# Half of the gate and up projections of two FFNs by seven half products instead of eight, on one Trainium2 core

## The chip, the cores and the metric

The kernel runs on one core of one Trainium2 chip. The metric is the device time of one execution in microseconds (us), a median over runs. One further execution was profiled; every duration and every row below is from that one. Engines are named as the profile names them: PE (TensorE, matmuls), PEld (its weight loads, which overlap the matmuls), DVE (VectorE), ACT (ScalarE), POOL (GpSimd) and SP (SyncE, which here only issues the DMAs).

## The reference, cut to what matters

Two layers, each a mixer and then a SwiGLU feed-forward network (FFN); the change is in the FFNs, which have 1024 model columns, 2816 inner columns and 512 tokens.

```python
def swiglu(h, w1, w3, w2):
    return (jax.nn.silu(h @ w1) * (h @ w3)) @ w2

for layer in range(DEPTH):                 # DEPTH = 2
    ...
    x = x + mix.astype(x.dtype)
    h = rmsnorm(x, norm_ffn_g[layer])
    x = x + swiglu(h, ffn_w1[layer], ffn_w3[layer], ffn_w2[layer]).astype(x.dtype)
```

All of it is float32.

## The kernel before

Activations are kept transposed: `xT[k]` holds 128 model columns (partitions) by 512 tokens, k = 0 to 7. A float32 product is made of three reduced-precision matmuls: each operand is split into a rounded part (`hh`, `whi`, `gh`: a cast on ACT, L116 for weights, L154 for activations) and what is left (`hl`, `wlo`, `gl`: a subtraction on DVE, L118 and L155), and PE adds wh·xh, wh·xl and wl·xh (L129, L130, L131). The RMS norm's factor per token, `R`, is applied after the projection.

The inner columns of an FFN are 22 tiles of 128, f = 0 to 21. For each f there is a pair of projections, the gate `a` and the up `b`. The weights of each come as one DMA of 512 KB into a buffer `raw` (two buffers for both), are split in two pieces of 512 columns into `whi` and `wlo` (five buffers each), and are multiplied in 8 blocks of 128 x 128 against 512 tokens, so 24 matmuls of 512 columns for `a` and 24 for `b`. Then come `ta` = a·R (DVE, L259), its silu (ACT, L260), `g` = b·ta (DVE, L262), g·R (POOL, L263) and the split of g into `gh` and `gl`. `ta` and `g` are in the shared temporaries of tag "t", of which there are four.

The 22 pairs go in two halves of 11. After each half, `residual_out` multiplies its 11 g tiles by `w2` for all 8 output tiles m and adds the result to `xT[m]` (L238); what the trace calls `y` is this. In the last FFN the last output tile is done in two parts of 256 tokens, the only 256-column matmuls against these operands.

The order of instructions on each engine is set by a scheduler that works on the whole program; each engine then runs its list in order, and waits at each instruction for what it needs. The functions that the diff touches follow.

Of the kernel before, what the change touches and what calls it, by code (L numbers as in the profile page):

```python
# [24 lines left out]
NF = DFF // 128  # L25
# [6 lines left out]
def trunk(ctx, tc, t_in, out):  # L32
    nc = tc.nc
    main = ctx.enter_context(tc.tile_pool(name="main", bufs=1))
    wp = ctx.enter_context(tc.tile_pool(name="wp", bufs=2))
# [16 lines left out]
    def temp(name, dt=F32):
        return tmp.tile([128, 512], dt, name=name, tag="t")
# [69 lines left out]
    def accumulate(o, ws, width, xs, first, last, j0=0):  # L123
        n = len(xs)
        for j, (xh, xl) in enumerate(xs):
            hi, lo = ws[(j0 + j) * width // 512]
            c = (j0 + j) * width % 512
            wh, wl = hi[:, c:c + width], lo[:, c:c + width]
            mm(o, wh, xh, start=first and j == 0, stop=False)  # L129
            mm(o, wh, xl, start=False, stop=False)  # L130
            mm(o, wl, xh, start=False, stop=last and j == n - 1)  # L131

    def project(src, name, width=128, tag="mm"):
        o = bank(tag, f"p_{name}")
# [91 lines left out]
    def residual_out(wsrc, k0, k1, xs, norm, name, tail=None):  # L226
        for m in range(KT):
            o = bank("sc" if m % 2 else "mm", f"{name}{m}")
            ws = []
            for c0 in range(k0, k1, 8):  # L230
                n = min(8, k1 - c0)
                ws.append((c0, n, load_split(wsrc[m, :, c0 * 128:(c0 + n) * 128], n * 128, f"{name}{m}_{c0}")))
            parts = [slice(0, S)] if tail is None or m < KT - 1 else [slice(0, 256), slice(256, 512)]
            for cs in parts:
                for c0, n, w in ws:
                    accumulate(o[:, cs], w, 128, [(a[:, cs], b[:, cs]) for a, b in xs[c0:c0 + n]],
                               c0 == k0, c0 + n == k1)
                nc.vector.tensor_tensor(out=xT[m][:, cs], in0=o[:, cs], in1=xT[m][:, cs], op=ALU.add)  # L238
                if norm is not None:
                    norm.take(m, cs)  # L240
                    if tail is not None:
                        norm.scale(m, cs)
                if len(parts) > 1:
                    tail(cs)

    def ffn(layer, norm, norm_next, tail=None):
        w13, w2 = t_in["w13"], t_in["w2"]
        bh = [slab(i, f"gh{layer}_{i}", FR) for i in range(2)]
        bl = [slab(2 + i, f"gl{layer}_{i}", FR) for i in range(2)]
        gs = [(bh[f // 4][:, f % 4, :], bl[f // 4][:, f % 4, :]) for f in range(8)]  # L250
        gs += [(cell(2 * f - 16, f"gh{layer}_{f}", FR), cell(2 * f - 15, f"gl{layer}_{f}", FR))
               for f in range(8, NF)]
        for f0, f1 in ((0, NF // 2), (NF // 2, NF)):
            for f in range(f0, f1):
                a = project(w13[layer, 2 * f], f"a{layer}_{f}")
                R = norm.R if norm.R is not None else norm.factor()
                b = project(w13[layer, 2 * f + 1], f"b{layer}_{f}", tag="sc")
                ta = temp(f"ta{layer}_{f}")
                nc.vector.tensor_tensor(out=ta, in0=a, in1=R, op=ALU.mult)  # L259
                nc.scalar.activation(out=ta, in_=ta, func=AF.Silu)  # L260
                g = temp(f"g{layer}_{f}")
                nc.vector.tensor_tensor(out=g, in0=b, in1=ta, op=ALU.mult)  # L262
                nc.gpsimd.tensor_tensor(out=g, in0=g, in1=R, op=ALU.mult)  # L263
                split(*gs[f], g)
# [27 lines left out]
    ws = load_split(w0[5], D, "v1")  # L292
# [697 lines left out]
```

## Time and profile before

| what | value |
|---|---|
| median of 3 runs | 1332.17 us (1331.62 to 1332.23) |
| profiled execution, its own time | 1332.36 us |
| its span, first to last instruction | 1330.6 us |
| TensorE clock granted, mean | 0.999 of full speed |
| PE busy | 1317.5 us (99%) |
| PEld busy | 1102.5 us (83%) |
| DVE busy | 706.0 us (53%) |
| ACT busy | 523.1 us (39%) |
| POOL busy | 357.4 us (27%) |

The time is the span and 1.8 us around it. Busy shares are averages over the whole span; the first FFN lies at about 306 to 670 us of it, the second at about 958 to 1324 us.

### The profile page before, as it was taken

The numbers are of one execution on the slowest core, as the hardware profiler recorded it, in microseconds if no ns is written. First come the engines' busy times: TensorE is split into PE (matmuls) and PEld (weight loads), VectorE is DVE, ScalarE is ACT, GpSimd is POOL, SyncE is SP. The second block draws the span as 40 slices with busy tenths as digits, with TensorE's granted clock in tenths as the row PEclk, the third lists the DMA queues.
The fourth block names the chain that finished last, engine by engine and source line by source line (L and its number), as shares of the span: only waits on it lengthen the run. The fifth ranks groups of instructions, "written<-read, shape, count | busy, mean of one in ns | idle before, by whom it ended". The sixth has DMA issues, their size and how long they took to land.

```text
span 1330.6 us, 17637 instructions
## 1 busy us (share of the span) xinstructions
PE 1317.5 (99%) x6593; PEld 1102.5 (83%) x6593; DVE 706.0 (53%) x1252; ACT 523.1 (39%) x975; POOL 357.4 (27%) x373
## 2 busy tenths in 40 slices
PE   9999999999999999999999999999999999999998
PEld 8888888888888888888888888888788888888887
DVE  6637776854444334444469777764744433344432
ACT  5346656543333223333343344332533322333343
POOL 0116676321111001111147665551211100011111
PEclk9999999999999999999999999999999999999999
DMA  7741111032333343323322212221323323333332
GB/s 260 179 139 49 32 49 48 17 101 90 95 98 94 89 147 96 95 85 103 97 80 89 71 56 72 64 67 61 111 82 99 104 83 110 95 96 95 92 93 85
DMA packets 40373, 121.95 MB, mean 92 GB/s; under 512 B 5408, under 2 KB 9952, under 8 KB 40160
## 3 DMA queue, kind: packets, MB, share of 16 engines
q1 hardware_dynamic: 40144, 120.57, 29.7%
q8 instruction: 52, 0.85, 0.3%
q10 hardware_dynamic: 144, 0.26, 0.1%
q14 instruction: 33, 0.27, 0.1%
HBM read 113.47 MB, written 2.10 MB: 87 GB/s over the span
## 4 chain that ended last, share of the span: by engine, by line
PE 80%; DVE 1%; issue 1%; POOL 1%; ACT 0%; POOLq 0%; DVEq 0%; ACTq 0%
PE p_b L129 6%; PE p_b L131 6%; PE p_a L131 6%; PE p_a L129 6%; PE p_a L130 6%; PE p_b L130 6%; PE y L129 6%; PE y L130 6%; PE y L131 6%; PE mo L129 2%; PE mo L130 2%; PE mo L131 2%; PE lv L787 2%; PE p_hg L130 1%; PE p_hg L131 1%; PE p_hg L129 1%
## 5 line engine op out<-in xcount | busy, mean ns | idle before, releaser
L263 POOL TENSOR_TENSOR g<-g,R 128x512 f32<-128x512 f32 x44 | 70.0, 1592 | 517.8 <-DVE g L262 517.8
L129 PE MATMUL y<-gh,whi_y 128*128 128x512 f32 (+1 forms) x363 | 139.0, 383 | 0.0
L131 PE MATMUL y<-gh,wlo_y 128*128 128x512 f32 (+1 forms) x363 | 138.3, 383 | 0.0
L130 PE MATMUL y<-gl,whi_y 128*128 128x512 f32 (+1 forms) x363 | 138.2, 383 | 0.0
L129 PE MATMUL p_b<-hh,whi_b 128*128 128x512 f32 x352 | 137.1, 390 | 0.0
L130 PE MATMUL p_a<-hl,whi_a 128*128 128x512 f32 x352 | 137.1, 390 | 0.0
L131 PE MATMUL p_b<-hh,wlo_b 128*128 128x512 f32 x352 | 137.0, 389 | 0.0
L129 PE MATMUL p_a<-hh,whi_a 128*128 128x512 f32 x352 | 136.9, 389 | 0.0
L131 PE MATMUL p_a<-hh,wlo_a 128*128 128x512 f32 x352 | 136.9, 389 | 0.0
L130 PE MATMUL p_b<-hl,whi_b 128*128 128x512 f32 x352 | 136.9, 389 | 0.0
L118 DVE TENSOR_TENSOR wlo_y<-raw_y,whi_y 128x512 fp32r<-128x512 f32 (+1 forms) x96 | 62.6, 652 | 95.9 <-ACT whi_y L116 95.9
L116 ACT CAST whi_y<-raw_y 128x512 fp32r<-128x512 f32 (+1 forms) x96 | 56.3, 586 | 144.1 <-PE y L130 102.0
L118 DVE TENSOR_TENSOR wlo_b<-raw_b,whi_b 128x512 fp32r<-128x512 f32 x88 | 62.8, 714 | 87.4 <-ACT whi_b L116 87.3
L116 ACT CAST whi_b<-raw_b 128x512 fp32r<-128x512 f32 x88 | 54.6, 621 | 125.5 <-issue 56.4
L116 ACT CAST whi_a<-raw_a 128x512 fp32r<-128x512 f32 x88 | 54.5, 619 | 98.7 <-PE p_b L130 71.1
L130 PEld LDWEIGHTS y<-gl,whi_y 128*128 128x128 f32 x363 | 68.2, 188 | 13.4
L129 PEld LDWEIGHTS y<-gh,whi_y 128*128 128x128 f32 x363 | 68.2, 188 | 13.3
L131 PEld LDWEIGHTS y<-gh,wlo_y 128*128 128x128 f32 x363 | 68.2, 188 | 13.2
L131 PEld LDWEIGHTS p_b<-hh,wlo_b 128*128 128x128 f32 x352 | 66.1, 188 | 13.8
L130 PEld LDWEIGHTS p_b<-hl,whi_b 128*128 128x128 f32 x352 | 66.1, 188 | 13.7
L130 PEld LDWEIGHTS p_a<-hl,whi_a 128*128 128x128 f32 x352 | 66.1, 188 | 13.7
L129 PEld LDWEIGHTS p_a<-hh,whi_a 128*128 128x128 f32 x352 | 66.1, 188 | 13.7
(379 smaller groups left out, 2998.8 us busy)
## 6 DMA issues: line engine op xcount, KB each, us to landing
raw_a<-w SPq DMA_DIRECT2D x44, 512.0 KB, 3.5
raw_b<-w SPq DMA_DIRECT2D x44, 512.0 KB, 3.6
raw_y<-w SPq DMA_DIRECT2D x32, 512.0 KB, 3.5
raw_mo<-w_out SPq DMA_DIRECT2D x16, 512.0 KB, 3.7
raw_r<-w_in SPq DMA_DIRECT2D x12, 512.0 KB, 3.6
raw_y<-w SPq DMA_DIRECT2D x32, 192.0 KB, 2.4
raw_hf<-w_in SPq DMA_DIRECT2D x8, 512.0 KB, 3.6
raw_hq<-w_in SPq DMA_DIRECT2D x8, 512.0 KB, 3.5
```

What stands on the lines that cost most here:

```text
L116: nc.scalar.copy(hi[:, :m], part)
L118: lo_eng[c // 512 % len(lo_eng)].tensor_tensor(out=lo[:, :m], in0=part, in1=hi[:, :m].bitcast(F32), op=ALU.subtract)
L129: mm(o, wh, xh, start=first and j == 0, stop=False)
L130: mm(o, wh, xl, start=False, stop=False)
L131: mm(o, wl, xh, start=False, stop=last and j == n - 1)
L263: nc.gpsimd.tensor_tensor(out=g, in0=g, in1=R, op=ALU.mult)
L787: mm(s_[:M, c * 64:(c + 1) * 64].rearrange("p (a b) -> p a b", b=B), k[:, c * 128:c * 128 + M], q4[:, c * nb:(c + 1) * nb, 1, :], start=Tr ...
```

## The change

Of the 22 pairs of each layer, eleven (`SEVEN`) are computed in another way. The two weight tiles a and b (128 inner columns each) are cut along the contraction into a first and a second half (a1, a2, b1, b2: 4 blocks of 128 x 128 each), and the activations along the tokens into the first and second 256. The two-by-two product of halves is then made from seven products instead of eight (Strassen's identity in Winograd's form), each of 4 blocks against 256 tokens.

- `seven_operands`, once per layer ahead of f = 2, forms the sums and differences of activations that four of the seven products need, for k = 0 to 3: `x1` and `x2` (ACT), `xu` and `xw` (DVE, four operations of 256 columns) and their splits. It uses the same four temporaries "t".
- `seven_products`, for each f in `SEVEN`, loads both weight tiles, forms four sums of weight halves s1 to s4 (DVE, 128 x 512), splits seven weight operands where a pair split four, makes 7 x 12 = 84 matmuls of 256 columns, and puts the results together in operations of 256 columns. `p1` is copied by ACT.
- The gated activations of the second half of the FFN now go where those of the first half were, so `residual_out` counts its tiles from k0, `lraw` (a mask's staging area, loaded in the first FFN) moves from slab 0 to slab 4, and the place of `yout` changes.

```diff
-                    accumulate(o[:, cs], w, 128, [(a[:, cs], b[:, cs]) for a, b in xs[c0:c0 + n]],
+                    accumulate(o[:, cs], w, 128, [(a[:, cs], b[:, cs]) for a, b in xs[c0 - k0:c0 - k0 + n]],
...
+    SEVEN = [2, 4, 6, 8, 10, 11, 13, 15, 17, 19, 21]
+    def seven_operands(layer, which):
+        lo, hi = slice(0, 256), slice(256, 512)
+        xs = {1: [], 2: [], 3: [], 4: [], 5: [], 6: [], 7: []}
+        for k in range(4):
+            x1, x2 = temp(f"x1_{layer}_{k}"), temp(f"x2_{layer}_{k}")
+            for x, j in ((x1, k), (x2, k + 4)):
+                nc.scalar.activation(out=x, in_=xT[j], func=AF.Copy, scale=gains[:, which, j:j + 1])
+            u, w = temp(f"xu_{layer}_{k}"), temp(f"xw_{layer}_{k}")
+            tt = nc.vector.tensor_tensor
+            tt(out=u[:, lo], in0=x1[:, lo], in1=x1[:, hi], op=ALU.subtract)
+            tt(out=u[:, hi], in0=x2[:, hi], in1=u[:, lo], op=ALU.add)
+            tt(out=w[:, lo], in0=x2[:, lo], in1=u[:, hi], op=ALU.subtract)
+            tt(out=w[:, hi], in0=x1[:, hi], in1=x2[:, hi], op=ALU.subtract)
...
+            split(*U, u)
+            split(*W, w)
+            for i, part, cs in ((1, (hh[k], hl[k]), lo), (2, (hh[k + 4], hl[k + 4]), lo),
+                                (3, (hh[k + 4], hl[k + 4]), hi), (5, U, lo), (6, U, hi), (4, W, lo), (7, W, hi)):
+                xs[i].append((part[0][:, cs], part[1][:, cs]))
+        return xs
...
+        def product(i, o, first):
+            ((wh_, wl_),) = ws[i]
+            for j, (xh, xl) in enumerate(xs[i]):
+                wh, wl = wh_[:, j * 128:(j + 1) * 128], wl_[:, j * 128:(j + 1) * 128]
+                mm(o, wh, xh, start=first and j == 0, stop=False, skip_group_check=True)
+                mm(o, wh, xl, start=False, stop=False, skip_group_check=True)
+                mm(o, wl, xh, start=False, stop=j == 3, skip_group_check=True)
...
+        parts(1, a1)
+        tt(out=s1, in0=b1, in1=b2, op=ALU.add)
+        tt(out=s2, in0=s1, in1=a1, op=ALU.add)
+        o1 = bank("mm", f"p_w{name}")[:, lo]
+        product(1, o1, True)
+        nc.scalar.copy(p1, o1)
+        parts(6, s2)
+        o2 = bank("sc", f"p_x{name}")[:, lo]
+        product(6, o2, True)
+        parts(2, a2)
+        tt(out=v, in0=o2, in1=p1, op=ALU.subtract)
+        tt(out=s3, in0=a1, in1=b1, op=ALU.add)
+        product(2, o1, False)
+        parts(7, s3)
+        product(7, o2, False)
+        parts(5, s1)
+        tt(out=v7, in0=o2, in1=p1, op=ALU.subtract)
+        tt(out=s4, in0=s2, in1=a2, op=ALU.add)
+        o3 = bank("sc", f"p_z{name}")[:, lo]
+        product(5, o3, True)
+        parts(4, b2)
+        product(4, o2, False)
+        tt(out=g[:, hi], in0=v7, in1=o3, op=ALU.subtract)
+        parts(3, s4)
+        product(3, o3, False)
+        R = norm.R
+        tt(out=ta[:, lo], in0=o1, in1=R[:, lo], op=ALU.mult)
+        tt(out=g[:, lo], in0=o2, in1=p1, op=ALU.subtract)
+        tt(out=ta[:, hi], in0=o3, in1=v, op=ALU.subtract)
+        tt(out=ta[:, hi], in0=ta[:, hi], in1=R[:, hi], op=ALU.mult)
+        nc.scalar.activation(out=ta, in_=ta, func=AF.Silu)
+        tt(out=g, in0=g, in1=ta, op=ALU.mult)
+        nc.gpsimd.tensor_tensor(out=g, in0=g, in1=R, op=ALU.mult)
...
+                if f == 2:
+                    xs = seven_operands(layer, norm.which)
+                if f in SEVEN:
+                    g = seven_products(layer, f, xs, norm, SEVEN.index(f))
```

Two places of the engines' lists show where the new work stands. In the order lists, `g0_1` is the g of layer 0, f = 1; `wlo_s5_0_2` is the low part of the weight operand of product 5 of layer 0, f = 2; `xu_0_k` and `xw_0_k` are the temporaries of `seven_operands`, and `xu0_k_0` and `xu0_k_1` the rounded and the low part of xu (the number at the end of a name counts buffers).

The first place is DVE's list behind the last result of f = 1 of layer 0. Before, the weights of the next pairs were split there:

```order
L262 TENSOR_TENSOR g0_1_3668<-p_b0_1_3630,ta0_1_3665 128x512
L118 TENSOR_TENSOR wlo_a0_3_0_3756<-raw_a0_3_3752,whi_a0_3_0_3754 128x512
L155 TENSOR_TENSOR gl0_0_3471<-g0_1_3668,gh0_0_3469 128x512
L118 TENSOR_TENSOR wlo_a0_3_512_3760<-raw_a0_3_3752,whi_a0_3_512_3758 128x512
L259 TENSOR_TENSOR ta0_2_3743<-p_a0_2_3673,R1_3550 128x512
```

Now, from the same instruction on (its line is L360):

```order
L360 TENSOR_TENSOR g0_1_3646<-p_b0_1_3608,ta0_1_3643 128x512
L118 TENSOR_TENSOR wlo_s5_0_2_0_3805<-s_0_2_3727,whi_s5_0_2_0_3803 128x512
L260 TENSOR_TENSOR xu_0_0_3655<-x1_0_0_3651 128x256
L261 TENSOR_TENSOR xu_0_0_3655<-x2_0_0_3652,xu_0_0_3655 128x256
L118 TENSOR_TENSOR wlo_s4_0_2_0_3824<-raw_b0_2_3724,whi_s4_0_2_0_3822 128x512
L155 TENSOR_TENSOR gl0_0_0_3471<-g0_1_3646,gh0_0_0_3469 128x512
L155 TENSOR_TENSOR xu0_0_1_3662<-xu_0_0_3655,xu0_0_0_3661 128x512
L262 TENSOR_TENSOR xw_0_0_3656<-x2_0_0_3652,xu_0_0_3655 128x256
L263 TENSOR_TENSOR xw_0_0_3656<-x1_0_0_3651,x2_0_0_3652 128x256
L118 TENSOR_TENSOR wlo_s3_0_2_0_3841<-s_0_2_3727,whi_s3_0_2_0_3839 128x512
L260 TENSOR_TENSOR xu_0_1_3673<-x1_0_1_3669 128x256
L155 TENSOR_TENSOR xw0_0_1_3664<-xw_0_0_3656,xw0_0_0_3663 128x512
```

The operands of `seven_operands` have moved in behind `g0_1`, for k = 0 and the start of k = 1; k = 2 and 3 follow in the same manner. On PE, products 1 and 2 of f = 2, which need no such operand, come first, and then products 6 (into `p_x`) and 5 (into `p_z`) alternate, k by k:

```order
L298 MATMUL p_w0_2_3738<-hh7_81,wlo_s2_0_2_0_3771 128x256
L296 MATMUL p_x0_2_3756<-xu0_0_0_3661,whi_s6_0_2_0_3752 128x256
L296 MATMUL p_z0_2_3809<-xu0_0_0_3661,whi_s5_0_2_0_3803 128x256
L297 MATMUL p_x0_2_3756<-xu0_0_1_3662,whi_s6_0_2_0_3752 128x256
L298 MATMUL p_x0_2_3756<-xu0_0_0_3661,wlo_s6_0_2_0_3754 128x256
L297 MATMUL p_z0_2_3809<-xu0_0_1_3662,whi_s5_0_2_0_3803 128x256
L298 MATMUL p_z0_2_3809<-xu0_0_0_3661,wlo_s5_0_2_0_3805 128x256
L296 MATMUL p_x0_2_3756<-xu0_1_0_3679,whi_s6_0_2_0_3752 128x256
```

Before, PE had there the 48 matmuls of the pair f = 2 with operands that are long made; now each group of six stands behind the xu of its k.

The second place is DVE's list between a pair of seven products and the next one, here f = 4 and f = 6 of layer 0, with the plain pair f = 5 between them (the pattern repeats through both layers). Before, DVE did per pair four weight splits, ta, g and gl:

```order
L118 TENSOR_TENSOR wlo_b0_5_512_3951<-raw_b0_5_3943,whi_b0_5_512_3949 128x512
L262 TENSOR_TENSOR g0_4_3902<-p_b0_4_3864,ta0_4_3899 128x512
L118 TENSOR_TENSOR wlo_a0_6_0_3990<-raw_a0_6_3986,whi_a0_6_0_3988 128x512
L155 TENSOR_TENSOR gl0_1_3472<-g0_4_3902,gh0_1_3470 128x512
L118 TENSOR_TENSOR wlo_a0_6_512_3994<-raw_a0_6_3986,whi_a0_6_512_3992 128x512
L259 TENSOR_TENSOR ta0_5_3977<-p_a0_5_3907,R1_3550 128x512
L118 TENSOR_TENSOR wlo_b0_6_0_4025<-raw_b0_6_4021,whi_b0_6_0_4023 128x512
```

Now the stretch up to the low part of s5 of f = 6 reads:

```order
L118 TENSOR_TENSOR wlo_s1_0_6_0_4175<-raw_a0_6_4164,whi_s1_0_6_0_4173 128x512
L305 TENSOR_TENSOR s_0_6_4168<-s_0_6_4168,raw_a0_6_4164 128x512
L331 TENSOR_TENSOR ta0_4_3952<-p_z0_4_4031,t1_0_4_3950 128x256
L357 TENSOR_TENSOR ta0_5_4156<-p_a0_5_4086,R1_3528 128x512
L320 TENSOR_TENSOR s_0_6_4168<-s_0_6_4168,raw_a0_6_4164 128x512
L332 TENSOR_TENSOR ta0_4_3952<-ta0_4_3952,R1_3528 128x256
L118 TENSOR_TENSOR wlo_s6_0_6_0_4195<-s_0_6_4168,whi_s6_0_6_0_4193 128x512
L118 TENSOR_TENSOR wlo_s2_0_6_0_4212<-raw_a0_6_4164,whi_s2_0_6_0_4210 128x512
L118 TENSOR_TENSOR wlo_s7_0_6_0_4230<-s_0_6_4168,whi_s7_0_6_0_4228 128x512
L334 TENSOR_TENSOR g0_4_3953<-g0_4_3953,ta0_4_3952 128x512
L360 TENSOR_TENSOR g0_5_4159<-p_b0_5_4121,ta0_5_4156 128x512
L118 TENSOR_TENSOR wlo_s5_0_6_0_4246<-s_0_6_4168,whi_s5_0_6_0_4244 128x512
```

Directly ahead of these rows stand the two weight sums L304 and L314, which wait for the loads of f = 6; ahead of them L330 (256 columns) and the low part of the second piece of b of f = 5, after which that piece's `raw` buffer is free for b of f = 6. L334 and L360 are each followed on POOL by a multiplication of their g by R (L335, L361). What moved: thirteen operations of DVE now stand between the arrival of b of f = 6 and the low part of s5, where a low part before stood directly behind its own cast. On PE the matmuls of this stretch go in the order products 1, 6, 5, 2 and 7 of f, 22 of the 24 matmuls of a of f + 1, products 4 and 3 of f, the last two of a, and the 24 of b of f + 1.

## Rows read from the trace of the kernel before

**Rows 1.** Page, part 1: busy time, share of the span.

```profile
PE 1317.5 (99%) x6593; PEld 1102.5 (83%) x6593; DVE 706.0 (53%) x1252; ACT 523.1 (39%) x975; POOL 357.4 (27%) x373
```

**Rows 2.** Windows: from:to, length, busy of each engine, PEclk, DMA share, GB/s.

```profile
306.00:670.00 364.00, 364.00 (x1616) 301.63 (x1615) 152.40 (x232) 120.60 (x200) 43.83 (x29) 1.00 0.33 99
958.00:1324.00 366.00, 366.00 (x1680) 305.38 (x1678) 142.23 (x223) 120.78 (x200) 44.51 (x30) 1.00 0.31 93
```

**Rows 3.** Timeline of PE: one pair in 512-column matmuls (start us, duration us).

```profile
485.45 0.39 PE L129 MATMUL p_a<-hh,whi_a 128*128 128x512 f32 x1
485.67 0.39 PE L130 MATMUL p_a<-hl,whi_a 128*128 128x512 f32 x1
...
490.89 0.39 PE L129 MATMUL p_b<-hh,whi_b 128*128 128x512 f32 x1
...
496.33 0.39 PE L129 MATMUL p_a<-hh,whi_a 128*128 128x512 f32 x1
```

**Rows 4.** Timeline of PE: the first and the last of 23 matmuls of 256 columns.

```profile
1319.09 0.28 PE L130 MATMUL y<-gl,whi_y 128*128 128x256 f32 x1
...
1321.72 0.29 PE L131 MATMUL y<-gh,wlo_y 128*128 128x256 f32 x1
```

**Rows 5.** Timeline of DVE: one pair of the first FFN; idle before, releaser in brackets.

```profile
499.65 0.69 DVE L155 TENSOR_TENSOR gl<-g,gh 128x512 fp32r<-128x512 f32 x1 [1.84 <-ACT gh L154]
500.26 0.68 DVE L118 TENSOR_TENSOR wlo_a<-raw_a,whi_a 128x512 fp32r<-128x512 f32 x1
501.97 0.69 DVE L259 TENSOR_TENSOR ta<-p_a,R 128x512 f32<-128x512 f32 x1 [1.02 <-PE p_a L131]
...
505.17 0.69 DVE L118 TENSOR_TENSOR wlo_b<-raw_b,whi_b 128x512 fp32r<-128x512 f32 x1 [1.91 <-ACT whi_b L116]
```

**Rows 6.** Timeline of ACT, the same stretch.

```profile
504.51 0.62 ACT L116 CAST whi_b<-raw_b 128x512 fp32r<-128x512 f32 x1 [1.19 <-PE p_b L130]
...
509.88 0.62 ACT L154 CAST gh<-g 128x512 fp32r<-128x512 f32 x1 [2.03 <-POOL g L263]
510.41 0.61 ACT L116 CAST whi_a<-raw_a 128x512 fp32r<-128x512 f32 x1
```

**Rows 7.** Timeline of SP: the issue of a weight load.

```profile
505.89 0.33 SPq L109 DMA_DIRECT2D raw_b<-w  x1
```

**Rows 8.** Page, part 6: DMA issues, KB each, us from issue to landing.

```profile
raw_b<-w SPq DMA_DIRECT2D x44, 512.0 KB, 3.6
```

**Rows 9.** Groups by form: count, busy us, mean ns, idle before.

```profile
L238 DVE TENSOR_TENSOR xall<-y,xall 128x256 f32<-128x256 f32 x2 | 0.8, 424 | 6.4 <-PE y L131 6.4
L118 DVE TENSOR_TENSOR wlo_b<-raw_b,whi_b 128x512 fp32r<-128x512 f32 x88 | 62.8, 714 | 87.4 <-ACT whi_b L116 87.3
L260 ACT ACTIVATE ta<-ta 128x512 f32<-128x512 f32 x44 | 27.8, 632 | 13.4 <-DVE ta L259 13.3
```

**Rows 10.** Timeline of PE: first matmuls of f = 2, first FFN.

```profile
327.69 0.39 PE L129 MATMUL p_a<-hh,whi_a 128*128 128x512 f32 x1
```

**Rows 11.** Timeline of DVE at the start of the first FFN.

```profile
323.19 0.68 DVE L259 TENSOR_TENSOR ta<-p_a,R 128x512 f32<-128x512 f32 x1
323.79 1.40 DVE L118 TENSOR_TENSOR wlo_b<-raw_b,whi_b 128x512 fp32r<-128x512 f32 x1
...
327.89 0.69 DVE L262 TENSOR_TENSOR g<-p_b,ta 128x512 f32<-128x512 f32 x1 [1.27 <-PE p_b L131]
328.49 0.68 DVE L118 TENSOR_TENSOR wlo_a<-raw_a,whi_a 128x512 fp32r<-128x512 f32 x1
```

**Rows 12.** Timeline of POOL, the same stretch.

```profile
323.35 1.28 POOL L263 TENSOR_TENSOR g<-g,R 128x512 f32<-128x512 f32 x1 [9.52 <-DVE g L262]
328.66 1.67 POOL L263 TENSOR_TENSOR g<-g,R 128x512 f32<-128x512 f32 x1 [4.02 <-DVE g L262]
```

**Rows 13.** Windows at the end of the program, columns as in rows 2.

```profile
1324.00:1328.00 4.00, 0.08 (x1) 0.00 (x0) 1.41 (x3) 1.26 (x2) 0.69 (x1) 1.00 0.50 202
1328.00:1330.60 2.60, 0.00 (x0) 0.00 (x0) 0.00 (x0) 0.00 (x0) 0.00 (x0) 0.50 0.41 161
```

More of the change, by code (lines that the diff above doesn't have):

```diff
@@ L244, in residual_out @@
                     tail(cs)
+    SEVEN = [2, 4, 6, 8, 10, 11, 13, 15, 17, 19, 21]
[12 more added lines that the diff above has]
+            tt(out=w[:, hi], in0=x1[:, hi], in1=x2[:, hi], op=ALU.subtract)
+            U, W = ([cell(6 + 4 * k + 2 * j + i, f"x{n}{layer}_{k}_{i}", FR) for i in range(2)]
+                    for j, n in enumerate("uw"))
+            split(*U, u)
[4 more added lines that the diff above has]
+        return xs
@@ new lines, in seven_products, with parts @@
+    def seven_products(layer, f, xs, norm, n):
+        w13 = t_in["w13"]
+        lo, hi = slice(0, 256), slice(256, 512)
+        tt = nc.vector.tensor_tensor
+        name = f"{layer}_{f}"
+        ra, rb = (wp.tile([128, 1024], F32, name=f"raw_{x}{name}", tag="raw", bufs=2) for x in "ab")
+        nc.sync.dma_start(out=ra, in_=w13[layer, 2 * f])
+        nc.sync.dma_start(out=rb, in_=w13[layer, 2 * f + 1])
+        a1, a2, b1, b2 = ra[:, 0:512], ra[:, 512:1024], rb[:, 0:512], rb[:, 512:1024]
+        if n % 2:
+            s1, s2, s3, s4 = (cell(22 + j, f"s{j}_{name}") for j in range(4))
+        else:
+            q = slab(4, f"s_{name}")
+            s1, s2, s3, s4 = (q[:, j, :] for j in range(4))
+        ws = {}
+        def parts(i, src):
+            ws[i] = load_split(None, 512, f"s{i}_{name}", [src])
+        def product(i, o, first):
[5 more added lines that the diff above has]
+                mm(o, wl, xh, start=False, stop=j == 3, skip_group_check=True)
+        t1, t2 = cell(26, f"t1_{name}"), cell(27, f"t2_{name}")
+        p1, v, v7 = t1[:, lo], t1[:, hi], t2[:, lo]
+        ta, g = temp(f"ta{name}"), temp(f"g{name}")
+        parts(1, a1)
[31 more added lines that the diff above has]
+        nc.gpsimd.tensor_tensor(out=g, in0=g, in1=R, op=ALU.mult)
+        return g
@@ L246, in ffn @@
     def ffn(layer, norm, norm_next, tail=None):
         w13, w2 = t_in["w13"], t_in["w2"]
[L248 to L253, printed above, removed]
-            for f in range(f0, f1):
[L255 to L264, printed above, removed]
+        half = NF // 2
@@ new lines, in ffn @@
+        for f0, f1 in ((0, half), (half, NF)):
+            bh = [slab(i, f"gh{layer}_{f0}_{i}", FR) for i in range(2)]
+            bl = [slab(2 + i, f"gl{layer}_{f0}_{i}", FR) for i in range(2)]
+            gs = [(bh[j // 4][:, j % 4, :], bl[j // 4][:, j % 4, :]) for j in range(8)]
+            gs += [(cell(2 * j, f"gh{layer}_{f0}_{j}", FR), cell(2 * j + 1, f"gl{layer}_{f0}_{j}", FR))
+                   for j in range(half - 8)]
+            for f in range(f0, f1):
+                if f == 2:
+                    xs = seven_operands(layer, norm.which)
+                if f in SEVEN:
+                    g = seven_products(layer, f, xs, norm, SEVEN.index(f))
+                else:
+                    a = project(w13[layer, 2 * f], f"a{layer}_{f}")
+                    R = norm.R if norm.R is not None else norm.factor()
+                    b = project(w13[layer, 2 * f + 1], f"b{layer}_{f}", tag="sc")
+                    ta = temp(f"ta{layer}_{f}")
+                    nc.vector.tensor_tensor(out=ta, in0=a, in1=R, op=ALU.mult)
+                    nc.scalar.activation(out=ta, in_=ta, func=AF.Silu)
+                    g = temp(f"g{layer}_{f}")
+                    nc.vector.tensor_tensor(out=g, in0=b, in1=ta, op=ALU.mult)
+                    nc.gpsimd.tensor_tensor(out=g, in0=g, in1=R, op=ALU.mult)
+                split(*gs[f - f0], g)
@@ L685, in trunk @@
     lmask = tmp.tile([128, 8, 256], U8, name="lmask", tag="pct", bufs=2)
-    lraw = slab(0, "lraw").rearrange("p a b -> p (a b)")[:, 0:2048]
+    lraw = slab(4, "lraw").rearrange("p a b -> p (a b)")[:, 0:2048]
     nc.sync.dma_start(out=lraw, in_=t_in["lmask"].rearrange("p a b -> p (a b)"))
@@ L882, in finish @@
         c0, c1 = cs.start // 128, cs.stop // 128
-        y = slab(c0 // 2, f"yout{c0}").rearrange("p (c e) n -> p c (e n)", e=2)
+        y = slab(0 if c0 else 4, f"yout{c0}").rearrange("p (c e) n -> p c (e n)", e=2)
         banks = {(c, e): bank("oo" if e and c % 2 == 0 else "sc" if e else "mm", f"yt{c}_{e}")
```

## The prediction

> **What bounds the kernel now.** I read the page's busy shares first: PE is busy 99% of the span [rows 1]. The windows over the two FFNs say where the change stands: in both PE has no idle at all, at full granted clock, while DVE works 152.40 of 364 us and 142.23 of 366, ACT a third, POOL an eighth [rows 2]. So a matmul less is time less, as long as every other engine keeps up; and nothing else that is made cheaper there would show. Then the timelines: each matmul of 512 columns is drawn 0.39 us long, but they overlap, so the pace is read from starts. A pair begins at 485.45, its b at 490.89, the next pair at 496.33 [rows 3]: 10.88 us for 48, 0.2267 each. The same operands in 256-column matmuls start at 1319.09 and, 22 steps on, at 1321.72 [rows 4]: 0.1195 each.
>
> **What the change removes on PE.** Per pair 48 matmuls at 0.2267 (10.88 us) become 84 at 0.1195 (10.04 us): 0.84 us less, and 18.4 us for 22 pairs. One eighth of the products goes, but 256 columns cost 53% of 512, not half; that takes 0.52 of the 1.36 us. If nothing ever waited, 1332.4 (the profiled execution; 0.2 over the median) would become 1314.0, and that is the bound of the gain.
>
> The Trainium skill ("TensorE: Matmul & The Clock Gate", section "Back-to-back issue gap") gives an isolated gap of columns/2.4 + 2.5 ns: by estimate 109 and 216 ns, where the rows have 119.5 and 226.7. By it the saving would be 1.18 us per pair and 26 us in all. The rows were measured on this kernel's operands and decide.
>
> **What it adds at f = 2, twice (once per layer).** Before, PE began f = 2 at 327.69 [rows 10]; I walk the new program from there in the first FFN. PE does products 1 and 2 (2.9 us), which need no new operand, and then products 6 and 5, which for each k wait for xu of that k and its low part. If all were ready, the four products would end 48 x 0.1195 = 5.74 us on, at 333.4. But xu and xw use the temporaries that f = 0 and f = 1 held, and stand on DVE behind g of f = 1 (order rows at the first place), which cannot start before b of f = 1 ends: 327.89 [rows 11].
>
> Durations: DVE 512 columns 0.69 with the next start 0.60 behind (499.65 and 500.26 [rows 5]); 256 columns 0.42 [rows 9], so about 0.34 to the next; ACT 0.62 with 0.53 [rows 6]. The low part of s5 starts at 328.5. POOL's multiplication of that g was put at 328.66, behind a DVE operation, and took 1.67 [rows 12], so to 330.33. The first xu operation reads only SBUF, and such an operation does not run beside POOL: wlo_b, begun at 323.79 with POOL at work from 323.35, took 1.40 instead of 0.68, while ta, which reads PSUM, took its usual 0.68 [rows 11, 12]. So xu of k = 0 begins at about 330.3 and is whole at 331.0. The low parts of s4, xu 0 and s3, gl and xw fill DVE to 334.1; xu of k = 1 is whole at 335.4.
>
> From there each k takes this: cast of xu on ACT (0.05 after it, 0.53), x1 of the next k in the temporary just left (0.62), the first xu operation (0.34), the low part of xw, which stands ahead of the second one (0.60), and that (0.34): 2.7 us with the handovers. So k = 3 is whole at 340.9, its cast at 341.6, its low part at 342.3, and the last matmuls of products 6 and 5 end at 342.8. Product 7 writes the bank that v is still to be taken from, and v stands behind the low part of xw of k = 3: 343.9, instead of 333.9 with two matmuls of a between. That is 10 us of PE per layer, 20 for both. The bound from below is DVE's own work, 4 x (4 x 0.34 + 2 x 0.60) = 10.2 us from 329.1 on, so 6 us of stall; from above, every operation behind the other at full duration, 4.5 us per k: 16 us. So 12 to 32 for both layers; I take the walk, 20, since it follows the lists.
>
> **What it adds in the rest, 18 times.** From f = 2 on, the order is a period of one seven-product pair and one plain pair: 10.04 + 10.88 = 20.92 us of PE. DVE's work in one: 4 sums, 7 + 4 low parts, L334, ta and g of the plain pair and two gl, 20 operations at 0.60, and 7 of 256 at 0.34: 14.4 us. Add 2 x 1.28 in which POOL holds the reads [rows 12]: 17.0 of 20.92. It fits, but not freely: it is a loop. With t = 0 at the start of product 1, a's first piece is done at 5 x 1.434 + 2.72 = 9.9; its whi buffer is the one that the cast of b's second piece waits for: cast 0.62, low part 0.69 (they follow within 0.05 us, 504.51 and 505.17 [rows 5, 6]), and SP issues the next load directly behind (505.89 [rows 7]), as the `raw` buffer comes free at 11.3. Landing takes 3.6 us [rows 8]: 14.9. Then the thirteen operations that the order rows at the second place show or name, eleven at 0.60 and two at 0.34, 7.3 us: the low part of s5 runs from 22.2 to 22.9. PE wants it in the third matmul of product 5: 20.92 + 24 x 0.1195 + 0.24 = 24.0. Slack: 1.1 us.
>
> POOL takes that. L334 ends at 21.7 and POOL's multiplication runs to 23.05; the low part of s5 waits for it and ends at 23.75, 0.25 before its time. POOL's second one (of the plain pair) comes next; it runs to 25.0 and pushes the low parts of s4 and s3, two gl and the next a to 28.5, where PE wants a at 28.6. From there the loop closes in just about its period. A stall of PE there is not hidden; it comes 4 times in a layer's first half and 5 in its second, 18 in all. Bounds: 0, and, if POOL's second operation takes the reads before s5, 1.28 us minus 0.25: 1.03 each, 18.5 in all. The nearest rows say that who comes first goes first (POOL at 328.66, 0.17 behind a DVE operation, took 1.67), and s5 comes first here, so I take 0.3, as 0.1 here or there goes straight into the sum: 5.4 us.
>
> The Trainium skill ("SBUF — State Buffer", section "Who interferes with whom") says that a VectorE operation with two SBUF inputs contends with a GpSimd operation that reads SBUF, that the loser waits for the whole of it, and that one with a single SBUF input doesn't. The 1.40 and the 0.68 us agree; were there no such lock, the sum would be lower by 1.2 us per layer and by the 5.4, at 1331.6.
>
> **What costs nothing.** ACT's three casts and the copy more per seven-product pair (2.0 us of 20.92, with ACT a third busy). At f = 10 and 21 the first y takes the place of a, in the same order. The reuse of the slabs moves lraw's load behind the first loads of the second half; its 1 MB and the cast stand beside PE work that is ready, and where that cover is gone cost 1 us once. The g tiles of the second half are written when the first half's y matmuls are over, by several us.
>
> **Sum.** 1332.4 - 18.4 + 20 + 5.4 = 1339.4; I say 1340.
>
> **The rivals.** A, the forecast: both stalls about as walked, 1335 to 1346; chance 0.47.
>
> B: the loop keeps its time and only f = 2 costs, 8 to 10 us per layer: 1330 to 1335. For it: arrival order, 3.9 us spare on DVE. Against: 0.25 us of slack where POOL stands between. 0.20, of which 0.12 within 0.2% of before (2.7 us, about what a measurement of this kernel can tell), 0.03 below.
>
> C: POOL's second operation gets the reads first, or a load lands later than 3.6 us; every period pays about 1 us: 1332.4 - 18.4 + 20 + 18.5 = 1352.5. Spread 1346 to 1357; 0.14.
>
> D, the other side: xu and xw are ready sooner than walked. It decides at one place, the wait of products 6 and 5 at f = 2; at its lower bound of 6 us per layer and with a clean loop the time is 1332.4 - 18.4 + 12 = 1326, and with nothing left of the wait 1314. The kernel is faster once both waits together stay under 15.7 us. For it: PE could start k = 0 at 331. Against: x1 of the next k needs the temporary of this one, so the chain cannot run ahead. 0.15.
>
> E: the clock. At f = 2 PE has only six matmuls in each 2.7 us. The granted clock is 1.00 in all windows with work; in the last one it is 0.50, the 1.2 GHz level, after PE had done a single instruction in the 4 us before [rows 13]. At half the clock a matmul of 512 columns would go at about 0.45 us instead of 0.2267 [rows 3], an estimate. If the level falls in the stall and some 13 matmuls go so, that is 3 us per layer; 22 cost 5: with A 1346 to 1350. 0.04.
>
> The Trainium skill ("TensorE: Matmul & The Clock Gate", section "HAM oscillation — how this bites in real kernels") states that stretches in which the array idles lower the clock; only the end of this trace agrees, and no row shows a sparse stretch.
>
> **Chances and range.** Faster: D and a little of B, 0.18. Same: 0.12. Slower: 0.70. The range from 1327 to 1355 leaves out most of D and the top of C, under 0.2; the likeliest one's own is 1335 to 1346.
>
> **What would show it.** PE idle at f = 2 of each layer, 10 us, put down to ACT or DVE on xu; PE idle under 0.5 us before product 5 in each period, put down to the low part of s5, with DVE subtractions of 1.3 us beside POOL; 256-column starts 0.12 apart; granted clock 1.00. Wrong if xu of k = 3 comes before 338, or if stalls stand elsewhere, above all at the weight sums (a later load).

## The result: 1340.05 us, and where the time went

| | before | with the change |
|---|---|---|
| median | 1332.20 us (1331.62 to 1332.23, 4 runs) | 1340.05 us (1339.44 to 1340.69, 4 runs) |
| ratio, 95% interval | | 1.006 (1.0047 to 1.0072): slower by 0.6% |
| profiled execution, its span | 1332.36, 1330.6 us | 1340.04, 1338.3 us |
| PE busy | 1317.5 us (99%) | 1312.1 us (98%) |
| DVE busy | 706.0 us (53%) | 886.2 us (66%) |
| mean granted clock | 0.999 | 0.990 |

The forecast was 1340, and slower. It hit the total, but not by its own terms, as follows.

PE is busy 5.4 us less and the span is 7.7 us longer, so PE waits. The windows over the two FFNs, which had no idle before [rows 2], with the changed kernel (columns as there):

```profile
306.00:672.00 366.00, 359.46 (x2003) 315.19 (x2002) 242.05 (x398) 149.61 (x259) 41.91 (x29) 0.99 0.32 98
960.00:1332.00 372.00, 365.39 (x2081) 322.20 (x2079) 234.77 (x392) 151.32 (x262) 44.18 (x32) 0.98 0.30 94
```

The timeline of PE says where. These are the first matmuls of f = 2, 4 and 6 in the first FFN and of f = 2 and 4 in the second:

```profile
327.17 0.28 PE L296 MATMUL p_w<-hh,whi_s 128*128 128x256 f32 x1
...
360.24 0.28 PE L296 MATMUL p_w<-hh,whi_s 128*128 128x256 f32 x1
...
381.24 0.28 PE L296 MATMUL p_w<-hh,whi_s 128*128 128x256 f32 x1
...
984.20 0.28 PE L296 MATMUL p_w<-hh,whi_s 128*128 128x256 f32 x1
...
1018.08 0.28 PE L296 MATMUL p_w<-hh,whi_s 128*128 128x256 f32 x1
```

A period of one seven-product and one plain pair takes 21.00 us (360.24 to 381.24), and so do all later ones in both layers; two plain pairs took twice 10.88, 21.76 [rows 3]. That is 0.76 us per seven-product pair, 16.7 for 22. But f = 2 and 3 take 33.07 us in the first layer and 33.88 in the second: 12.07 and 12.88 too much, 24.95 together. 24.95 - 16.7 = 8.2; the first FFN's f = 2 began 0.5 us earlier (327.17 against 327.69 [rows 10]); that leaves the 7.7.

What waits at f = 2, in PE's timeline (idle before and its releaser in brackets):

```profile
329.88 0.39 PE L296 MATMUL p_w<-hh,whi_s 128*128 128x256 f32 x1 [1.12 <-ACT t L308]
...
332.46 0.39 PE L297 MATMUL p_x<-xu,whi_s 128*128 128x256 f32 x1 [0.64 <-DVE xu L155]
...
335.85 0.39 PE L296 MATMUL p_x<-xu,whi_s 128*128 128x256 f32 x1 [2.65 <-ACT xu L154]
...
341.59 0.58 PE L296 MATMUL p_x<-xu,whi_s 128*128 128x256 f32 x1 [0.92 <-ACT xu L154]
...
344.62 0.41 PE L296 MATMUL p_x<-xw,whi_s 128*128 128x256 f32 x1
...
346.52 0.28 PE L296 MATMUL p_x<-xw,whi_s 128*128 128x256 f32 x1
```

The first of these waits is product 2's, for ACT's copy of p1; it ends before the first cast of xu does (331.25), so nothing hangs on it. The others are the waits for xu.

And on DVE, the first and the last operands:

```profile
328.58 1.49 DVE L260 TENSOR_TENSOR xu<-x 128x256 f32<-128x256 f32 x1
330.17 0.42 DVE L261 TENSOR_TENSOR xu<-x,xu 128x256 f32<-128x256 f32 x1
...
340.45 0.43 DVE L261 TENSOR_TENSOR xu<-x,xu 128x256 f32<-128x256 f32 x1
...
341.57 0.69 DVE L155 TENSOR_TENSOR xu<-xu,xu 128x512 fp32r<-128x512 f32 x1
```

The chain is the one that was walked: the first xu operation beside POOL takes 1.49 instead of 0.42 us, and xu is whole at 330.59 for k = 0 and at 340.88 for k = 3 (walked 331.0 and 340.9 from a start 0.52 us later). In PE's rows something else shows: from 336.6 on the matmuls are drawn 0.41 and 0.58 us long, not 0.28, until 346.52. The windows (PEclk is the third number from the end):

```profile
327.17:336.50 9.33, 4.78 (x33) 3.96 (x31) 8.93 (x16) 7.66 (x14) 1.64 (x1) 0.99 0.31 104
336.50:346.50 10.00, 8.02 (x27) 6.49 (x28) 7.91 (x17) 5.81 (x10) 0.00 (x0) 0.50 0.06 9
346.50:360.24 13.74, 13.74 (x75) 11.88 (x74) 9.66 (x18) 4.79 (x8) 0.65 (x1) 1.00 0.24 76
```

The granted clock is 0.50, the 1.2 GHz level, for 10 us, after a stretch in which PE's own busy time was 4.78 of 9.33 us. In the second layer the waits are the same, but the level stays low for longer, 12.5 us, and that is why 12.88 us are lost there and not 12.07:

```profile
992.80:1005.30 12.50, 10.48 (x35) 8.55 (x36) 9.45 (x21) 7.16 (x13) 0.00 (x0) 0.50 0.15 43
```

In the steady state, DVE and POOL around the low part of s5 (403.45) look like this; L304 is the first use of the landed b:

```profile
396.15 0.69 DVE L304 TENSOR_TENSOR s<-raw_b 128x512 f32<-128x512 f32 x1 [0.64 <-DMA raw_b<-w]
...
402.85 0.68 DVE L360 TENSOR_TENSOR g<-p_b,ta 128x512 f32<-128x512 f32 x1
403.45 1.40 DVE L118 TENSOR_TENSOR wlo_s<-s,whi_s 128x512 fp32r<-128x512 f32 x1
404.77 1.78 DVE L118 TENSOR_TENSOR wlo_s<-raw_b,whi_s 128x512 fp32r<-128x512 f32 x1
```

```profile
403.00 1.29 POOL L335 TENSOR_TENSOR g<-g,R 128x512 f32<-128x512 f32 x1 [17.98 <-DVE g L334]
404.25 1.75 POOL L361 TENSOR_TENSOR g<-g,R 128x512 f32<-128x512 f32 x1
```

```profile
405.36 0.28 PE L298 MATMUL p_z<-xu,wlo_s 128*128 128x256 f32 x1
```

The period began at 381.24, so L304 stands at 14.91 (walked 14.9). In these rows the low parts and POOL's multiplications take turns in the order in which they came. s5 is done at 404.85, and PE, in product 5 from 405.12 on, takes it at 405.36 without a wait: half a microsecond to spare.

### The profile page after: what moved, and what is told of

The parts are those of the page before. It is cut to its first block, busy times and chain, and to the rows that moved or that the text cites. A ratio compares the mean times of both kernels' runs of the same rounds, so it can differ in the third digit from the quotient of the medians.

```text
span 1338.3 us, 19686 instructions
## 1 busy us (share of the span) xinstructions
PE 1312.1 (98%) x7385; PEld 1132.7 (85%) x7385; DVE 886.2 (66%) x1586; ACT 581.6 (43%) x1095; POOL 353.6 (26%) x373
## 4 chain that ended last, share of the span: by engine, by line
PE 78%; DVE 2%; ACT 1%; issue 1%; POOL 1%; POOLq 0%; DVEq 0%; ACTq 0%
PE y L130 6%; PE y L129 6%; PE y L131 6%; PE p_a L129 3%; PE p_a L130 3%; PE p_a L131 3%; PE p_b L129 3%; PE p_b L130 3%; PE p_b L131 3%; PE p_x L296 2%; PE p_x L297 2%; PE p_x L298 2%; PE mo L129 2%; PE mo L130 2%; PE mo L131 2%; PE lv L885 2%
## 5 line engine op out<-in xcount | busy, mean ns | idle before, releaser
L335 POOL TENSOR_TENSOR g<-g,R 128x512 f32<-128x512 f32 x22 | 29.0, 1320 | 516.7 <-DVE g L334 516.7
L116 ACT CAST whi_s<-s 128x512 fp32r<-128x512 f32 x88 | 54.4, 618 | 90.7 <-DVE s L305 63.1
L118 DVE TENSOR_TENSOR wlo_s<-s,whi_s 128x512 fp32r<-128x512 f32 x88 | 71.6, 814 | 3.7 <-ACT whi_s L116 3.6
L129 PE MATMUL p_a<-hh,whi_a 128*128 128x512 f32 x176 | 69.8, 396 | 0.1
L130 PE MATMUL p_a<-hl,whi_a 128*128 128x512 f32 x176 | 69.6, 395 | 0.0
L131 PE MATMUL p_a<-hh,wlo_a 128*128 128x512 f32 x176 | 68.9, 391 | 0.0
L129 PE MATMUL p_b<-hh,whi_b 128*128 128x512 f32 x176 | 68.7, 390 | 0.0
L130 PE MATMUL p_b<-hl,whi_b 128*128 128x512 f32 x176 | 68.6, 390 | 0.0
L131 PE MATMUL p_b<-hh,wlo_b 128*128 128x512 f32 x176 | 68.6, 390 | 0.0
L600 POOL TENSOR_TENSOR P<-P,st 128x128 f32<-128x128 f32 (+3 forms) x64 | 45.7, 737 | 34.7 <-DVE st L598 25.9
L895 POOL TENSOR_TENSOR hk<-hk,hT 128x256 f32<-128x256 f32 x48 | 42.3, 887 | 44.0 <-PE lv L885 40.6
```

The source lines that it names most:

```text
L116: nc.scalar.copy(hi[:, :m], part)
L118: lo_eng[c // 512 % len(lo_eng)].tensor_tensor(out=lo[:, :m], in0=part, in1=hi[:, :m].bitcast(F32), op=ALU.subtract)
L600: nc.gpsimd.tensor_tensor(out=Ps[x][:, 0:n], in0=Ps[x][:, 0:n], in1=st[:, 6 + x:7 + x].to_broadcast([128, n]), op=ALU.mult)
L895: nc.gpsimd.tensor_tensor(out=k4[:, :, 0, :], in0=k4[:, :, 0, :], in1=t2[:, :, 1:2].to_broadcast([128, npair, B]), op=ALU.mult)
```

## The experiments

Theory 1: all that is lost is the wait for xu at f = 2 and the clock that falls in it; the wait comes from the chain's start behind f = 1, in shared temporaries. Its rivals: the operands' work is too much wherever it stands; the loss is in the reuse of the space; the steady state has room on DVE that could be used (or has none).

**own_buffers** (and **own_buffers_again**): x1, x2, xu and xw get buffers of their own.

```diff
-            x1, x2 = temp(f"x1_{layer}_{k}"), temp(f"x2_{layer}_{k}")
+            x1, x2 = cell(22, f"x1_{layer}_{k}"), cell(23, f"x2_{layer}_{k}")
...
-            u, w = temp(f"xu_{layer}_{k}"), temp(f"xw_{layer}_{k}")
+            u, w = cell(24, f"xu_{layer}_{k}"), cell(25, f"xw_{layer}_{k}")
```

> Only the four temporaries x1, x2, xu, xw of seven_operands are changed: they get four buffers of their own (cells 22 to 25, free until f = 4) and no longer share those of ta and g. In the program's lists their work then stands among the weight splits of f = 0 and 1. Theory 1 (all that is lost is the wait for xu at f = 2, and it comes from the start of the chain, which the shared temporaries put behind g of f = 1): f = 2 and 3 take 21.0 us of TensorE as all later periods do, instead of 33.1 and 33.9, so 1340.05 - 12.1 - 12.9 = 1315.1 us, 1313.5 to 1317. Rival (the 24 VectorE and 16 ScalarE operations are simply too much work in this place and push out weight splits wherever they stand): the stall moves to f = 0 and 1, 4 us or more per layer, 1323 us or more.

1317.83 us, ratio to before 0.9895 (0.9878 to 0.9911); again 1317.77. So 22 us came back by two changed lines: far from the rival, and 0.8 us above the range of theory 1. f = 2 and 3 take 21.00 us in the first layer. The chain itself is no shorter than before; it only starts earlier. Its first operation and the end of xu of k = 3 are 13.9 us apart (300.82 to 314.70), where the change took 12.3 (328.58 to 340.88):

```profile
300.82 1.07 DVE L260 TENSOR_TENSOR xu<-x 128x256 f32<-128x256 f32 x1 [0.38 <-ACT x L257]
...
314.28 0.42 DVE L261 TENSOR_TENSOR xu<-x,xu 128x256 f32<-128x256 f32 x1
```

The 2.7 us that are missing to 1315.1 are in the second layer, whose operands now run beside the mixer's output projection: there a late matmul of a of f = 0 waits for hh (the expectation of held_operands below calls it the first one of the FFN, which it is not), DVE meets POOL, and at f = 2 the low part of s5 is late.

```profile
956.63 0.50 PE L129 MATMUL p_a<-hh,whi_a 128*128 128x512 f32 x1 [1.00 <-ACT hh L170]
...
977.72 0.38 PE L298 MATMUL p_z<-xu,wlo_s 128*128 128x256 f32 x1 [0.57 <-DVE wlo_s L118]
```

```profile
951.21 1.80 DVE L171 SCALAR_TENSOR_TENSOR hl<-xall,gains,hh 128x512 fp32r<-128x512 f32 x1
```

**held_operands** and **held_by_last_x** start the operands later: the scale of x1 and x2 is read from a small tile that depends on a of f = 0, or on the last tile of x.

```diff
+                        held = main.tile([128, KT], F32, name=f"held{layer}", tag="held", bufs=1)
+                        nc.vector.scalar_tensor_tensor(out=held, in0=a[:, 0:KT], scalar=0.0,
+                                                       in1=gains[:, norm.which, :], op0=ALU.mult, op1=ALU.add)
```

> own_buffers, with x1 and x2 held back until a of f = 0 is done (their scale is taken from a small tile that VectorE makes from it), so that the operands of the second layer no longer run beside the mixer's output projection, where own_buffers shows the first matmul of its FFN waiting 1.0 us for hh and VectorE operations of 1.45 and 1.80 us beside GpSimd. Theory (that collision is the 1.8 us by which own_buffers came out above the sum, together with 0.8 us at its f = 2): 1.5 to 2.6 us less than own_buffers, 1315.2 to 1316.5. Rival (own_buffers is at its limit, and the later start brings a wait for xu back): 1317.5 us or more.

> own_buffers once more, on the same chip as held_operands, for their difference: 1317.8 us within 0.8.

own_buffers_again gave 1317.77 us, and held_operands 1321.77, 4.0 above it (ratio to before 0.992, 0.9908 to 0.9932): the theory's total missed, and the time lies where the rival put it. The mechanism was half seen: the stretch from the second mixer's start to f = 2 is back from 317.9 to 316.1 us, but each f = 2 waits again, 23.9 and 24.0 us instead of 21.0 (327.77 to 351.70 in the first layer). For held_by_last_x, `in0` is `xT[KT - 1][:, 0:KT]`.

> held_operands, with the small tile made from the last column tile of x instead of from a of f = 0: the operands of a layer start when the mixer's output projection is over, some 5 us earlier than in held_operands. Theory (held_operands showed two things at once: the stretch between the layers back at 316.1 from 317.9 us, as expected, and 2.9 us of wait at each f = 2 from the late start): both go, f = 2 and 3 take 21.0 to 21.4 us and the stretch between 316.1, so 1315.2 to 1316.6. Rival (the early operands collide with the splits of f = 0 and 1 too): 1317.5 us or more.

1315.31 us, ratio 0.9872 (0.9856 to 0.9888): as expected, 0.2 from the 1315.1 that the account above gives without the loss at f = 2. Both f = 2 are clean; the first, in PE's timeline:

```profile
327.50 0.28 PE L296 MATMUL p_w<-hh,whi_s 128*128 128x256 f32 x1
...
348.50 0.28 PE L296 MATMUL p_w<-hh,whi_s 128*128 128x256 f32 x1
```

**from_four**: the operands as in the change, but the first pair that needs them is f = 4.

```diff
-    SEVEN = [2, 4, 6, 8, 10, 11, 13, 15, 17, 19, 21]
+    SEVEN = [4, 6, 8, 10, 11, 13, 15, 17, 19, 21]
```

> The first seven-product pair is f = 4; f = 2 is a plain pair; ten seven-product pairs per layer instead of eleven. The operands are made with the shared temporaries as before, from f = 2 on, so their chain of 11 us lies beside two plain pairs (21.8 us of TensorE). Theory 1: no stall; 20 pairs at 0.76 us off 1332.2 give 1317.0 us, 1315 to 1319. Rival (the operands' work stalls TensorE wherever it stands): as much stall as in the change, 1337 us or more.

1321.50 us, ratio 0.9921 (0.9906 to 0.9936): f = 4 and 5 take 21.13 and 21.26 us, so the operands' work as such is hidden, but the time is 4.5 us above the theory's 1317.0, 2.5 above its range. By the trace nearly all of that is lost in one place, which was no part of the theory: the cast of lraw stands on DVE ahead of the last low part of f = 20, and waits for its load.

```profile
575.32 0.69 DVE L118 TENSOR_TENSOR wlo_b<-raw_b,whi_b 128x512 fp32r<-128x512 f32 x1
579.57 1.23 DVE L786 CAST lmask<-lraw 128x2048 uint8<-128x2048 f32 x1 [3.56 <-DMA lraw<-lmask]
580.71 0.68 DVE L118 TENSOR_TENSOR wlo_b<-raw_b,whi_b 128x512 fp32r<-128x512 f32 x1
```

```profile
593.72 0.39 PE L298 MATMUL p_z<-xu,wlo_s 128*128 128x256 f32 x1 [2.00 <-DVE wlo_s L118]
```

The next load of b starts 3.5 us late, and the low part of s5 reaches PE 2.0 us too late. Here, too, the clock falls behind the wait, for 3.2 us, in which a matmul of 256 columns takes 0.21 us; that adds 1.5 us:

```profile
594.36:597.57 3.21, 3.21 (x17) 3.21 (x17) 3.21 (x6) 1.24 (x2) 0.45 (x1) 0.50 0.22 66
```

In the change itself that cast stands beside the y matmuls and costs nothing.

**reuse_only**: no seven-product pair, only the reuse of the space.

```diff
-    SEVEN = [2, 4, 6, 8, 10, 11, 13, 15, 17, 19, 21]
+    SEVEN = []
...
-                if f == 2:
+                if f == 2 and SEVEN:
```

> No pair by seven products; only the second edit is left, that the g tiles of the second half reuse the space of the first and that lraw and yout change their slabs. Both theories on f = 2 expect no change here, 1332.2 us within 1; a rival to them, that reuse of the slabs makes the second half wait for the first half's y matmuls or for lraw, expects 1 us or more above.

1332.92 us, ratio 1.0006 (0.9996 to 1.0015): no difference that can be told.

**warm_clock**: PE gets work in the stall; nothing reads its results.

```diff
             split(*U, u)
+            if k < 3:
+                d = bank("tr", f"warm{layer}_{k}")[:, lo]
+                for j in range(16):
+                    mm(d, hh[k][:, 0:128], U[0][:, lo], start=j == 0, stop=j == 15, skip_group_check=True)
```

> The change with 16 further matmuls of 256 columns behind each of the first three casts of xu, into a bank that nothing reads: TensorE has work in the stall, its results are not used. Theory (the second part of the loss at f = 2 is the clock: granted 0.50 from 336.5 to 346.5, in which the seventh product took 2.3 instead of 1.4 us): the level stays at 1.00 and 2 us per layer come back, 1336 us, 1334.5 to 1337.5. Rival (the lower level costs nothing, as TensorE waits for VectorE anyway): 1340 us or, with the added matmuls in the way, more.

1337.28 us, 2.8 below the change, in the theory's range. The clock stays:

```profile
327.21:336.50 9.29, 6.52 (x52) 6.10 (x51) 8.88 (x16) 7.62 (x14) 1.65 (x1) 1.00 0.30 104
336.50:346.50 10.00, 9.50 (x67) 8.45 (x66) 9.24 (x21) 6.50 (x11) 0.00 (x0) 1.00 0.08 16
```

f = 2 and 3 take 31.52 us in both layers (327.21 to 358.73 in the first), 1.55 and 2.36 less than in the change: 3.9 us of the 24.95 are the clock, the rest the wait (with the added matmuls in its gaps). The median gained 2.8 and not 3.9, as f = 4 and 5 of the first layer then take 21.73 us and not 21.00; product 5 of f = 4 waits for the low part of s5:

```profile
358.73 0.28 PE L300 MATMUL p_w<-hh,whi_s 128*128 128x256 f32 x1
...
362.46 0.39 PE L302 MATMUL p_z<-xu,wlo_s 128*128 128x256 f32 x1 [0.46 <-DVE wlo_s L118]
...
380.46 0.28 PE L300 MATMUL p_w<-hh,whi_s 128*128 128x256 f32 x1
```

**factor_on_dve**: for f = 1, g is multiplied by R on DVE.

```diff
-                    nc.gpsimd.tensor_tensor(out=g, in0=g, in1=R, op=ALU.mult)
+                    (nc.vector if f == 1 else nc.gpsimd).tensor_tensor(out=g, in0=g, in1=R, op=ALU.mult)
```

> The change with the multiplication of g by R for f = 1 on VectorE instead of GpSimd, so that no GpSimd operation is at work when the first xu operation starts. Theory (that operation took 1.49 us instead of 0.42 for GpSimd's sake, and everything at f = 2 hangs on it): the first xu operation takes 0.42 and ends about 0.5 us earlier, as the multiplication now takes 0.6 of VectorE ahead of it; f = 2 and 3 take 0.5 us less in each layer, 1339 us. Rival (the wait is not GpSimd's doing): the first xu operation is as long as before or ends 0.6 us later, 1340 to 1341.5 us.

1338.71 us, 1.3 below the change; the first operands on DVE:

```profile
329.12 0.42 DVE L260 TENSOR_TENSOR xu<-x 128x256 f32<-128x256 f32 x1
329.54 0.69 DVE L118 TENSOR_TENSOR wlo_s<-raw_b,whi_s 128x512 fp32r<-128x512 f32 x1
330.14 0.42 DVE L261 TENSOR_TENSOR xu<-x,xu 128x256 f32<-128x256 f32 x1
```

The operation takes 0.42 and ends at 329.54 instead of 330.07, as expected; but another low part moved in ahead of L261, which starts where it did (330.14, before 330.17). f = 2 and 3 take 32.81 us in the first layer, 0.26 less than in the change, and 32.21 in the second, 1.67 less. In the second, the granted clock is low for 9.3 us where the change had 12.5:

```profile
992.20:1001.50 9.30, 7.32 (x23) 5.57 (x24) 8.59 (x17) 6.53 (x12) 0.00 (x0) 0.50 0.00 1
```

So the total near the theory's 1339 does not confirm its 0.5 us per layer. What the multiplication beside it cost is shown for the operation, not for the chain.

**two_more_sums**: own_buffers with 1.2 us more of DVE in each period.

```diff
         tt(out=s1, in0=b1, in1=b2, op=ALU.add)
+        tt(out=s1, in0=b1, in1=b2, op=ALU.add)
+        tt(out=s1, in0=b1, in1=b2, op=ALU.add)
```

> own_buffers with the sum s1 made three times over in each seven-product pair (the same values again): two more VectorE operations of 128 x 512, 1.2 us per period of two pairs, ahead of s2. Theory (the period is a loop through the raw buffers: from the arrival of b's weights thirteen operations lead to the low part of s5, which in the change's trace ends 0.5 us before TensorE wants it): 0.7 us of stall in each of 18 periods, 12.6 us above own_buffers, 1326 to 1334. Rival (VectorE is free 3.5 of 21.0 us in a period, so 1.2 more is hidden): 1318 us as own_buffers.

1342.35 us, 24.5 above own_buffers and above the theory's range: 1.36 us for each of the 18 periods, where the theory had 0.7. The rival's hidden work is refuted. In the trace the first period of each half takes at most 0.13 us more than in own_buffers, the later ones 22.2 to 22.4 us, 1.2 to 1.4 more: the delay is handed on from period to period. A period, and two gaps of the next one:

```profile
370.95:393.22 22.27, 21.75 (x133) 19.23 (x132) 18.24 (x30) 9.03 (x17) 3.29 (x2) 1.00 0.32 95
```

```profile
396.21 0.28 PE L297 MATMUL p_z<-xu,whi_s 128*128 128x256 f32 x1
396.69 0.38 PE L296 MATMUL p_w<-hh,whi_s 128*128 128x256 f32 x1 [0.19 <-ACT t L310]
...
398.09 0.28 PE L298 MATMUL p_w<-hh,wlo_s 128*128 128x256 f32 x1
398.70 0.39 PE L298 MATMUL p_z<-xu,wlo_s 128*128 128x256 f32 x1 [0.33 <-DVE wlo_s L118]
```

DVE is busy 18.24 of 22.27 us, and yet PE waits for it: it is the loop that is full, not the engine. The order of the lists changed too (product 2 now stands inside product 5), so why it is 1.2 to 1.4 and not 0.7 is open. The rows also show how idle is to be read: 396.21 to 396.69 is 0.48 where the pace is 0.12, so 0.36 is lost, and the view says 0.19, since a matmul is drawn 0.28 long.

**all_seven** and **two_of_three**: own_buffers with more seven-product pairs.

```diff
+    SEVEN = list(range(2, 22))
...
+    SEVEN = [2, 3, 5, 6, 8, 9, 11, 12, 14, 15, 17, 18, 20, 21]
```

> own_buffers with all pairs from f = 2 to 21 by seven products, 20 per layer. Theory (VectorE and the two raw buffers bound such a pair: 13 operations at 0.60, 7 at 0.34 and 0.9 beside GpSimd make 11.1 us against TensorE's 10.08, and the load of the next b waits for the low part of s4, the last but one of the pair, with 3.6 us to land): 11.1 to 13 us per pair, slower than the kernel before: 1341 to 1415 us. Rival (TensorE stays the bound): 40 pairs at 0.76 to 0.8 us off, 1302 us.

> own_buffers with two seven-product pairs to each plain pair, 14 per layer. Theory (raw buffers and VectorE as in all_seven, but every third pair gives time back): some us of stall where two such pairs follow each other, 10 times, 2 to 4 us each: 1332 to 1355 us. Rival (VectorE's sum over three pairs, 28.6 of 31.0 us, is what counts): 6 more pairs at 0.76 us off 1317.8, 1313 us.

1374.66 us (1.0315, 1.0299 to 1.0330) and 1331.25 us (0.9993, 0.9983 to 1.0003). All by seven: 12.4 us per pair (379.06 to 391.50), DVE busy in nine tenths:

```profile
343.50:428.70 85.20, 75.16 (x591) 71.59 (x589) 77.37 (x140) 38.53 (x70) 10.19 (x7) 1.00 0.27 85
```

So PE, busy 75.16 of 85.20 us, is no longer the bound there. Two of three lose 1.5 us in each group of three pairs (32.5, 342.85 to 375.38, instead of 31.0), more than the six further pairs save (4.6 us in all); the theory's range began 0.8 us above the result, the rival was 18 below.

## Why the prediction was right, and where it was not

The direction was right for the cause given: the wait for xu at f = 2 costs more than the seven products save. That the total was right to 0.05 us is luck, as the errors in its terms cancel: 1339.4 + 1.7 (saving) + 4.95 (wait) - 5.4 (loop) - 0.52 (f = 2 begins earlier) = 1340.1. By mechanism the run is rival B's clean loop, with a longer wait than its 8 to 10 us per layer, and rival E's fall of the clock; the forecast itself, A, had both stalls.

- **Saving on PE, 18.4 us:** measured 16.7. Products of 12 matmuls take 1.44 us, not 1.434 (381.24 to 388.44 is five), and a few hundredths per pair go where 256 columns change to 512. The gap that the Trainium skill gives for one isolated matmul ("TensorE: Matmul & The Clock Gate", section "Back-to-back issue gap"), columns/2.4 + 2.5 ns, would have made it 26 us; the runs decide against it here.
- **The wait at f = 2, 20 us:** measured 24.95. The chain came out as walked, within 0.5 us at each end. The step that failed is E: a fall of the clock got 0.04 and no place in the sum, and it happened, in both layers. It cost 3.9 us by warm_clock; 3 to 5 per layer had been its price, and 1.6 and 2.4 were measured. Without the clock the wait is 21.0 us by the same run, against the 20 walked.
- **The loop, 5.4 us:** measured 0. The walk itself had found 0.25 us of slack; the 0.3 of stall put on top was the error. In the rows of 403.00 to 404.77 the order of arrival decides between DVE and POOL, as in the nearest rows of before. That the loop is nearly full was right: two_more_sums paid for all of 1.2 us in each later period, where the prediction had counted 3.9 spare on DVE.
- **The read lock:** seen at 1.49, 1.40 and 1.78 us. The Trainium skill's rule ("SBUF — State Buffer", section "Who interferes with whom") agrees: a VectorE operation with two SBUF inputs waits until a GpSimd one that reads SBUF is done. That 1.2 us per layer hang on it at f = 2 is not shown.
- **Nothing for the reuse of the space:** right, by reuse_only. The cast of lraw cost more than the 1 us that was put down for it where its cover is gone: 4.5 us in from_four, 1.5 of them by the clock.
- **Rival D** named the deciding place, the wait at f = 2. But xu was not ready sooner than walked. own_buffers shows that the start of the chain, not its length, was what cost: its buffers were shared with the results of the pairs ahead.

## What to carry to other kernels

Work that is short beside a busy engine still costs its whole length if its buffers tie its start to the consumer's last step: look for whose buffer the first operation takes, and give a one-time preparation its own. Where matmuls are traded for vector work, walk one period as a loop through its buffers; the busy share of the vector engine tells too little. A stall of the matmul engine is charged twice when the clock falls in it, as in the change (3.9 us) and in from_four (1.5 us).

## What was not expected of the hardware

The granted clock fell to 0.50, the 1.2 GHz level, although the longest wait in PE's records at f = 2 was 2.65 us and a few matmuls stood between the waits; in from_four it fell after waits of 0.54 and 2.00 us with a dozen matmuls between. At f = 2 of the first layer product 7, which had all its operands, still went at 0.21 us a matmul; the level was back at 346.52, PE having worked without a gap since 343.60. In the second layer it stayed low for 12.5 us after the same waits. Sixteen further matmuls in each of three gaps kept it at 1.00 throughout.
